# One distance in SBUF between the packed matmul operands and the weights, a shifted last row tile in two of them, and five-bank PSUM for the first three MLP blocks

## The chip, the cores and the metric

The kernel runs on one core of a Trainium2 chip. The metric is the device time of one execution in microseconds (us); ns are nanoseconds. Engines are named as in the profile: PE is TensorE's matmul, PEld its weight load, DVE is VectorE, ACT is ScalarE, POOL is GpSimd, SP is SyncE, whose queue issues the weight DMAs.

## The reference

One decoder layer on 256 tokens and 16 prepended meta tokens, width 2048, in fp32. The parts that matter here:

```python
proj = xn @ w_in                    # xn = rmsnorm(h); 11 pieces: q, k, v of both mixers, gates
o_fox = forgetting_attention(...)   # 8 heads of 128: 1024 channels
o_gla = head_rmsnorm(gated_linear_attention(...)) * silu(gr)        # 2048 channels
y = sigmoid(gate_fox) * (o_fox @ w_o_fox) + sigmoid(gate_gla) * (o_gla @ w_o_gla)
h = h + y @ w_out
h = h + square(relu(rmsnorm(h) @ w_ff1)) @ w_ff2                    # d_ff = 8192
return rmsnorm(h)[:, 16:]
```

## The kernel before, in words

Activations lie transposed: 128 channels on the partitions, tokens along the row. A weight matrix is cut into blocks of 2048 input by 128 output channels (1 MB), and the blocks are streamed from HBM in the order in which they are used, in two halves of 8 row tiles of 128x128. Each half is copied by ACT to `whi` (rounded to TensorE's fp32r) and DVE writes the remainder `wlo` (L120, L121). Five buffers of 4096 bytes each serve `raw`, `whi` and `wlo`.

A product to fp32 accuracy takes three matmuls in fp32r: hi by hi, hi by the operand's remainder, remainder of the weights by hi. `gemm3` does so for one output block: 16 row tiles `k`, for each of them L144 (`whi`, operand half 0), L145 (`whi`, half 1), L146 (`wlo`, half 0). That is 48 matmuls with 256 columns and 48 weight loads, in one PSUM bank. The banks come from pool `pg` (three banks in turn); pool `px` (five banks) serves the small products.

Five operands of `gemm3` are made by `operand`: a row tile takes 512 floats (2048 bytes), the layout is row tile, token half, hi or remainder, 128 tokens. Argument `at` says at which float of the SBUF tile the packed data start. They live in two slots (tags `s1`, `s2`) and, for `of`, in pool `late`:

- `of`, 8 row tiles: attention's output; `og`, 16 row tiles: the linear attention's output. A loop over `j0` makes eight passes; a pass has four gate blocks (`gate`, with `gemm2` and the operand `x`, L136 and L137; for the first pass they come ahead of the loop), two blocks of 24 matmuls with `of`, two blocks of 48 with `og`.
- `y`, 16 blocks with `w_out`; each block's result is added to `h`, and from it row tile `j` of `x2` is made and squared for the second norm.
- MLP: four groups `g`; in each 16 blocks with `x2` (w_ff1), whose squared relu fills `a`, then 16 blocks with `a` (w_ff2). In the last group the last four blocks are done in another way (L917, L933).

`x2` holds h times the norm's gain but not its root: the squared relu `relu2` multiplies by `r2b` (L883), the root that `norm2` makes while the first MLP block runs. Until then the first results wait in their PSUM banks.

A scheduler sets the order of each engine's queue. On PE the `gemm3` blocks follow each other as in the source, but for the first pass, where it interleaves them, since the corners of `of` (the last 16 tokens of each half, `fill_corners`, L805 to L809) come late.

Of the kernel before, what the change touches and what calls it, by code (L numbers as in the profile page):

```python
# [7 lines left out]
F32 = mybir.dt.float32  # L8
F32R = mybir.dt.float32r
# [7 lines left out]
P = 128  # L17
D = 2048
KT = D // P
NM = 16  # L20
NT = 256
NA = NM + NT
EPS = 1e-6
FOX_H, FOX_D = 8, 128
# [10 lines left out]
O_FQ, O_FK, O_FV, O_FF = 0, 1024, 2048, 3072  # L35
O_GQ, O_GK, O_GV, O_GR = 3080, 4104, 5128, 7176
O_GA, O_GF, O_GG = 9224, 9240, 11288


def stream():  # L40
# [25 lines left out]
def trunk(ctx: ExitStack, tc: tile.TileContext, hT, w_small, w_all, consts, w_alpha2, out):  # L66
# [3 lines left out]
    def nm(s):  # L70
        serial[0] += 1
        return f"{s}_{serial[0]}"

    const = ctx.enter_context(tc.tile_pool(name="const", bufs=1))
    keep = ctx.enter_context(tc.tile_pool(name="keep", bufs=1))
# [3 lines left out]
    pg = ctx.enter_context(tc.tile_pool(name="pg", bufs=3, space=PSUM))  # L79
    px = ctx.enter_context(tc.tile_pool(name="px", bufs=5, space=PSUM))  # L80
# [3 lines left out]
    def bank(pool, s):  # L84
        return pool.tile([P, 512], F32, tag="bank", name=nm(s))
# [7 lines left out]
    def issued():  # L93
        for e in list(waiting):
            e[0] -= 1
            if e[0] <= 0:
                waiting.remove(e)
                e[1]()
# [9 lines left out]
    def weight_half(c, i, hi=None):  # L108

        raw = wp.tile([P, HK * P], F32, tag="raw", name=nm("raw"), bufs=RAW)  # L110
        if hi is None:
            hi = wp.tile([P, HK, P], F32R, tag="whi", name=nm("whi"))
        lo = wp.tile([P, HK, P], F32R, tag="wlo", name=nm("wlo"))

        def step(k0, n):
            k = slice(k0, k0 + n)
            cols = slice(k0 * P, (k0 + n) * P)
            nc.sync.dma_start(raw[:, cols], w_all[c][:, i * HK * P + cols.start : i * HK * P + cols.stop])
            r = raw.rearrange("p (k m) -> p k m", m=P)[:, k, :]
            nc.scalar.copy(hi[:, k, :], r)  # L120
            nc.vector.tensor_tensor(lo[:, k, :], r, hi[:, k, :].bitcast(F32), op=ALU.subtract)  # L121

        return hi, lo, step

    def next_weights(keep_hi=None):
        c = chunk[0]
        chunk[0] += 1
        parts = []
        for i in range(2):
            hi, lo, step = weight_half(c, i, None if keep_hi is None else keep_hi[:, HK * i : HK * (i + 1), :])  # L130
            step(0, HK)
            parts.append((hi, lo))
        return lambda k: (parts[k // HK][0][:, k % HK, :], parts[k // HK][1][:, k % HK, :])
# [2 lines left out]
        nc.tensor.matmul(ps, hi, x, start=first, stop=False)  # L136
        nc.tensor.matmul(ps[:, 0:NT], lo, x[:, 0, :], start=False, stop=last)  # L137

    def gemm3(w, x, k0=0, nk=KT):

        ps = bank(pg, "ps")[:, 0:NT]
        for k in range(nk):
            hi, lo = w(k0 + k)
            nc.tensor.matmul(ps, hi, x[:, k, 0], start=(k == 0), stop=False)  # L144
            nc.tensor.matmul(ps, hi, x[:, k, 1], start=False, stop=False)  # L145
            nc.tensor.matmul(ps, lo, x[:, k, 0], start=False, stop=(k == nk - 1))  # L146
        issued()
        return ps

    def gemm2(w, x, k0=0, nk=KT):  # L150

        ps = bank(pg, "ps")
        for k in range(nk):
            hi, lo = w(k0 + k)
            mac2(ps, hi, lo, x[:, k], k == 0, k == nk - 1)
        issued()
        return ps

    def gemm_all(w):

        ps = bank(pg, "psa")
        for k in range(KT):
            hi, lo = w(k)
            nc.tensor.matmul(ps[:, 0:NA], hi, x_hi[:, k], start=(k == 0), stop=False)  # L164
            nc.tensor.matmul(ps[:, 0:NA], lo, x_hi[:, k], start=False, stop=(k == KT - 1))  # L165
            nc.tensor.matmul(ps[:, X_LO], hi, x_lo[:, k], start=False, stop=(k == KT - 1), skip_group_check=True)  # L166
        join(ps)
        issued()
        return ps
# [6 lines left out]
    def total(ps, t=None):  # L176

        b = tmp.tile([P, NT], F32, tag="evb", name=nm("evb"))
        nc.scalar.copy(b, ps[:, NT:512])
        if t is None:  # L180
            t = tmp.tile([P, NT], F32, tag="evt", name=nm("evt"), bufs=4)
        nc.vector.tensor_tensor(t, ps[:, 0:NT], b, op=ALU.add)
        return t

    def split_to(dst_hi, dst_lo, src):
        nc.scalar.copy(dst_hi, src)
        nc.vector.tensor_tensor(dst_lo, src, dst_hi.bitcast(F32), op=ALU.subtract)
# [38 lines left out]
            nc.vector.scalar_tensor_tensor(r, r, -0.5, v, op0=ALU.mult, op1=ALU.mult)  # L226
            nc.vector.scalar_tensor_tensor(y, r, 1.5, y, op0=ALU.add, op1=ALU.mult)

    def operand(pool, name, nk=KT, at=0, **kw):

        t = pool.tile([P, nk * (2 * NT + 32)], F32R, name=nm(name), **kw)
        return t[:, at : at + nk * 2 * NT].rearrange("p (k a o t) -> p k o a t", a=2, o=2, t=P)

    def pair(ap):
        return ap.rearrange("p (a t) -> p a t", t=P)
# [6 lines left out]
    x = x_row[:, :, NM : NM + 2 * NT].rearrange("p k (o t) -> p k o t", t=NT)  # L242
# [3 lines left out]
    ident, scan = cons[:, 0:P], cons[:, P : P + NA]  # L246
    ggn, ba, bf = cons[:, 400:416], cons[:, 416:424], cons[:, 424:425]

    room = keep.tile([P, KT * 2 * NT], F32, tag="s2", name="room")
    at_room = [0]  # L250

    def take(*shape):
# [55 lines left out]
    def load_stage(s, part):  # L308
        c0, n = ((0, 4), (4, 3))[part]
        w = first_weights(c0, n, 2 * s)  # L310
        stages.setdefault(s, []).append(w)
        return w[2](0, n) if s else w[2]
# [14 lines left out]
    for s in range(KT // 2):  # L327
        if s + 3 < KT // 2:
            with tc.issue_after(load_stage(s + 3, 0).ins):
                load_h(nc.sync, 2 * s + 6, 2)  # L330
            last = load_stage(s + 3, 1).ins
        wa, wb = stages[s]
        for kk in range(2):
            k = 2 * s + kk
# [15 lines left out]
        at = [(w[0][:, c], w[1][:, c]) for w, n in ((wa, 4), (wb, 3)) for c in range(n)]  # L350
# [38 lines left out]
    for i in range(2):  # L389
        w = wp.tile([P, HK, P], F32R, tag="whi", name=nm("whi"))  # L390
# [269 lines left out]
    ps = bank(pg, "psa")  # L660
    for k in range(KT):
        if k == HK:
            norm1()
        w = small[k // HK][:, k % HK, :]
# [28 lines left out]
    cum.close()  # L693
    branches = ExitStack()
    late = branches.enter_context(tc.tile_pool(name="late", bufs=1, reuse_waits="tile"))
    of = operand(late, "of", FOX_H, 96)
    negc = late.tile([P, FOX_H, NA], F32, name="negc")
    nc.gpsimd.dma_start(negc.rearrange("p h t -> p (h t)"), fdram.to_broadcast([P, FOX_H * NA]))
    fox = ExitStack()
# [16 lines left out]
    def fox_head(hd):  # L716
        fk = att.tile([P, NA], F32, tag="fk", name=nm("fk"))
        fq = att.tile([P, NT], F32, tag="fq", name=nm("fq"))
        ps = gemm_all(next_weights())
        nc.vector.tensor_tensor(fk, ps[:, 0:NA], rb, op=ALU.mult)  # L720
        t = total(gemm2(next_weights(), x))
# [32 lines left out]
        ps = gemm_all(next_weights())  # L754
# [11 lines left out]
        vg, pgr, og4 = corner["v"], corner["p"], corner["o"]  # L766
# [38 lines left out]
        def fill_corners(pu, vz, pz):  # L805
            nc.tensor.matmul(pu[:, 2 * P : 3 * P], vz, pz, start=True, stop=True)
            nc.vector.tensor_tensor(og4, og4, pu[:, 2 * P : 3 * P].rearrange("p (h c q) -> p h c q", c=2, q=NM),
                                    op=ALU.add)
            split_to(*(of[:, hd - 3 : hd + 1, o, :, P - NM :] for o in range(2)), og4)  # L809

        later(1, turn_v)
        later(2, turn_p)
# [20 lines left out]
    for j0 in range(0, KT, 2):  # L833
        gates = ahead if j0 == 0 else [gate() for _ in range(4)]
        w = next_weights()
        for j in range(2):
            t = gemm3(w, of, k0=8 * j, nk=8)
            nc.vector.tensor_tensor(gates[2 * j], gates[2 * j], t, op=ALU.mult)
        for j in range(2):
            t = tmp.tile([P, NT], F32, tag="evt", name=nm("evt"), bufs=4)  # L840
            nc.vector.tensor_tensor(t, gates[2 * j + 1], gemm3(next_weights(), og), op=ALU.mult)
            nc.vector.tensor_tensor(yf[:, j0 + j, :], gates[2 * j], t, op=ALU.add)
    y = operand(keep, "y", at=96, tag="s1")
    for j in range(KT):
        split_to(y[:, j, 0], y[:, j, 1], pair(yf[:, j, :]))
    mix.close()
# [6 lines left out]
    x2 = operand(keep, "x2", at=64, tag="s2")  # L853

    def square_sum(j, acc):
        if j == 0:
            nc.scalar.activation(acc, ht[:, j, :], AF.Square)
        else:
            sq = gat.tile([P, NT], F32, tag="hsq", name=nm("hsq"))
            nc.scalar.activation(sq, ht[:, j, :], AF.Square)  # L860
            nc.gpsimd.tensor_tensor(acc, acc, sq, op=ALU.add)

    def add_residual(j, ps):
        nc.vector.tensor_tensor(ht[:, j, :], ps, ht[:, j, :], op=ALU.add)
# [16 lines left out]
    def relu2(a, f, ps):  # L881
        t = tmp.tile([P, NT], F32, tag="evt", name=nm("evt"), bufs=4)
        nc.vector.scalar_tensor_tensor(t, ps, 0.0, r2b, op0=ALU.max, op1=ALU.mult)  # L883
        s = gat.tile([P, NT], F32, tag="asq", name=nm("asq"))
        nc.vector.tensor_tensor(s, t, t, op=ALU.mult)
        split_to(a[:, f, 0], a[:, f, 1], pair(s))

    acc = gat.tile([P, NT], F32, tag="acc", name="acc3", bufs=1)
    for g in range(NG):
        a = operand(keep, "a", at=(96, 64, 80, 64)[g], tag="s1")  # L890
        held = []
        for f in range(KT):
            ps = gemm3(next_weights(), x2)
            if g == 0 and f == 0:
                held.append(ps)
                continue
            if g == 0 and f == 1:
                relu2(a, 0, held.pop())
            relu2(a, f, ps)
        last = g == NG - 1  # L900
        for j in range(KT - NL if last else KT):
            add_residual(j, gemm3(next_weights(), a))
            if last:
                square_sum(j, acc)
                nc.scalar.activation(ht[:, j, :], ht[:, j, :], AF.Identity, scale=gain(2, j))
                if j == 0:
                    tc.keep_in_program_order(nc.scalar.preload_act_table_set("natural_log_exp_and_others"))
# [5 lines left out]
    for n in range(NL):  # L913
        j, ps = KT - NL + n, bank(pg if n < 3 else px, "ps")
        w = next_weights(whi[:, n])
# [148 lines left out]
```

## Time and profile before

| | |
|---|---|
| median of 3 runs | 1590.02 us (1589.83, 1590.02, 1592.55) |
| the profiled execution's own time | 1592.38 us |
| its span | 1590.7 us, 30310 instructions |
| PE busy | 1580.0 us (99%), 12436 matmuls |
| PEld busy | 1533.7 us (96%), 12436 weight loads |
| DVE, ACT, POOL busy | 1003.6 us (63%), 747.1 us (47%), 126.9 us (8%) |
| HBM | 289.32 MB read, 183 GB/s over the span |
| granted TensorE clock | 0.998 |

Matmuls overlap in the trace: one of 256 columns is shown with some 280 ns, while the next starts some 115 ns after it. How fast PE goes is therefore read from how many matmuls start in a stretch of time, or from how long a stage with a known number of matmuls lasts, and not from the duration of one. The windows that are cut at the first matmul of a stage give this directly: 16 blocks of `gemm3` are 768 matmuls.

### The profile page before, as it was taken

The page shows a single profiled execution, that of the slowest core. Times are in us where ns is not written, and L with a number is a line of the kernel's source. Part 1 is how long each engine was busy: PE and PEld are TensorE (multiplying, and loading weights), DVE is VectorE, ACT ScalarE, POOL GpSimd, SP SyncE. Part 2 cuts the span into 40 slices and gives each one's busy share as a digit, 9 for nine tenths or more (in the row PEclk, how much of TensorE's full clock was granted, in tenths as well). Part 3 has the DMA queues.
Part 4 walks back from the last instruction along what each step waited for, and adds up shares of the span by engine and source line. Part 5 has one row for each costly group of instructions (what it writes and reads, how often), then busy time and mean ns, then how long its engine had stood idle before and what let it go on. Part 6 is the DMA issues. An engine that isn't in the chain of part 4 may idle for free.

```text
span 1590.7 us, 30310 instructions
## 1 busy us (share of the span) xinstructions
PE 1580.0 (99%) x12436; PEld 1533.7 (96%) x12436; DVE 1003.6 (63%) x1487; ACT 747.1 (47%) x1099; POOL 126.9 (8%) x213
## 2 busy tenths in 40 slices
PE   9999999999999999999999999999999999999997
PEld 8999999999999999999999999999999999999997
DVE  7897757676665555555666765556655665556655
ACT  7665444455544444444544443344433443344553
POOL 6021000011100000000011000000000000000022
PEclk9999999999999999999999999999999999999999
DMA  9454545555545555556555555556656655556652
GB/s 325 153 167 151 182 159 179 167 188 165 164 162 183 188 193 190 189 187 194 188 187 186 186 186 186 186 190 195 195 192 197 192 193 185 184 188 196 192 184 106
DMA packets 86619, 293.41 MB, mean 184 GB/s; under 512 B 9112, under 2 KB 16800, under 8 KB 86352
## 3 DMA queue, kind: packets, MB, share of 16 engines
q1 hardware_dynamic: 85872, 289.62, 56.4%
q8 instruction: 98, 1.61, 0.4%
q0 software_dynamic: 176, 1.12, 0.2%
q10 hardware_dynamic: 432, 0.72, 0.1%
q14 instruction: 41, 0.34, 0.1%
HBM read 289.32 MB, written 2.11 MB: 183 GB/s over the span
## 4 chain that ended last, share of the span: by engine, by line
PE 98%; DMA 0%; DVE 0%; issue 0%; ACT 0%; POOL 0%; SPq 0%; POOLq 0%; ACTq 0%
PE ps L145 19%; PE ps L144 19%; PE ps L146 19%; PE ps L136 13%; PE ps L137 7%; PE psa L166 5%; PE psa L165 5%; PE psa L164 5%; PE ps L356 1%; PE ps L933 1%; PE ps L361 1%; PE pa L559 1%; PE ps L917 0%; DMA raw<-w_all_dram 0%; PE po L622 0%
## 5 line engine op out<-in xcount | busy, mean ns | idle before, releaser
L121 DVE TENSOR_TENSOR wlo<-raw,whi 128x1024 fp32r<-128x1024 f32 x522 | 640.9, 1228 | 420.1 <-ACT whi L120 411.0
L120 ACT CAST whi<-raw 128x1024 fp32r<-128x1024 f32 x522 | 548.5, 1051 | 699.9 <-PE ps L145 484.3
L136 PE MATMUL ps<-x,whi 128*128 128x512 f32 x928 | 326.9, 394 | 0.0
L144 PE MATMUL ps<-x,whi 128*128 128x256 f32 x1024 | 284.0, 277 | 0.5 <-DVE evt L883 0.5
L146 PE MATMUL ps<-x,wlo 128*128 128x256 f32 x1024 | 284.0, 277 | 0.0
L145 PE MATMUL ps<-x,whi 128*128 128x256 f32 x1024 | 284.0, 277 | 0.0
L145 PE MATMUL ps<-a,whi 128*128 128x256 f32 x960 | 268.0, 279 | 0.0
L146 PE MATMUL ps<-a,wlo 128*128 128x256 f32 x960 | 267.8, 279 | 0.0
L144 PE MATMUL ps<-a,whi 128*128 128x256 f32 x960 | 267.8, 279 | 0.0
L137 PE MATMUL ps<-x,wlo 128*128 128x256 f32 x928 | 261.0, 281 | 0.0
L136 PEld LDWEIGHTS ps<-x,whi 128*128 128x128 f32 x928 | 174.1, 188 | 37.0
L144 PEld LDWEIGHTS ps<-x,whi 128*128 128x128 f32 x1024 | 193.2, 189 | 0.6 <-issue 0.6
L145 PEld LDWEIGHTS ps<-x,whi 128*128 128x128 f32 x1024 | 192.3, 188 | 0.0
L146 PEld LDWEIGHTS ps<-x,wlo 128*128 128x128 f32 x1024 | 192.3, 188 | 0.0
L144 PEld LDWEIGHTS ps<-a,whi 128*128 128x128 f32 x960 | 181.5, 189 | 0.0
L164 PE MATMUL psa<-x,whi 128*128 128x272 f32 x624 | 181.4, 291 | 0.0
L145 PEld LDWEIGHTS ps<-a,whi 128*128 128x128 f32 x960 | 181.4, 189 | 0.0
L166 PE MATMUL psa<-x,whi 128*128 128x272 f32 x624 | 181.2, 290 | 0.0
L146 PEld LDWEIGHTS ps<-a,wlo 128*128 128x128 f32 x960 | 181.2, 189 | 0.0
L165 PE MATMUL psa<-x,wlo 128*128 128x272 f32 x624 | 179.5, 288 | 0.0
L137 PEld LDWEIGHTS ps<-x,wlo 128*128 128x128 f32 x928 | 175.3, 189 | 0.1
L164 PEld LDWEIGHTS psa<-x,whi 128*128 128x128 f32 x624 | 118.2, 189 | 0.4
(313 smaller groups left out, 2207.3 us busy)
## 6 DMA issues: line engine op xcount, KB each, us to landing
raw<-w_all_dram SPq DMA_DIRECT2D x537, 512.0 KB, 4.0
raw<-w_all_dram SPq DMA_DIRECT2D x8, 384.0 KB, 6.4
h<-hT_dram SPq DMA_DIRECT2D x8, 275.0 KB, 6.7
negc<-fdram POOLq DMA_DIRECT2D x1, 1088.0 KB, 8.4
out_dram<-o SPq DMA_DIRECT2D x2, 512.0 KB, 2.6
raw<-w_all_dram SPq DMA_DIRECT2D x2, 256.0 KB, 3.7
room<-w_small_dram SPq DMA_DIRECT2D x1, 320.0 KB, 7.7
out_dram<-o ACTq DMA_DIRECT2D x1, 320.0 KB, 3.1
```

What stands on the lines that cost most here:

```text
L120: nc.scalar.copy(hi[:, k, :], r)
L121: nc.vector.tensor_tensor(lo[:, k, :], r, hi[:, k, :].bitcast(F32), op=ALU.subtract)
L136: nc.tensor.matmul(ps, hi, x, start=first, stop=False)
L137: nc.tensor.matmul(ps[:, 0:NT], lo, x[:, 0, :], start=False, stop=last)
L144: nc.tensor.matmul(ps, hi, x[:, k, 0], start=(k == 0), stop=False)
L145: nc.tensor.matmul(ps, hi, x[:, k, 1], start=False, stop=False)
L146: nc.tensor.matmul(ps, lo, x[:, k, 0], start=False, stop=(k == nk - 1))
L164: nc.tensor.matmul(ps[:, 0:NA], hi, x_hi[:, k], start=(k == 0), stop=False)
L165: nc.tensor.matmul(ps[:, 0:NA], lo, x_hi[:, k], start=False, stop=(k == KT - 1))
L166: nc.tensor.matmul(ps[:, X_LO], hi, x_lo[:, k], start=False, stop=(k == KT - 1), skip_group_check=True)
L356: nc.tensor.matmul(ps, hi, x[:, k], start=st, stop=False)
L361: nc.tensor.matmul(ps[:, 0:NT], lo, x[:, k, 0], start=False, stop=sp)
```

## The change

Four edits, all in how tiles lie in memory.

1. `operand` takes as much room as it needs (`at` plus the row tiles, plus `kick`), where it took 32 spare floats for each row tile. With `kick=32` the last row tile starts 32 floats (128 bytes) further than the others. `Rows` hides this from the callers: index `k` picks the one access pattern or the other.
2. `at` and `kick` are set so that all rows stand at one distance from the weights. Here, a distance is the address of a matmul's moving operand less that of its weights, modulo 512 bytes; a weight tile's row is 512 bytes long and an operand's row tile 2048, so it is the same for all row tiles of an operand.

| operand | slot | `at` before, after | distance before, after (bytes) |
|---|---|---|---|
| `of` | `late` | 96, 96 | 192, 192; last row tile 320 |
| `og` | `s2` | 64, 64 | 192, 192 |
| `y` | `s1` | 96, 64 | 320, 192; last row tile 320 |
| `x2` | `s2` | 64, 64 | 192, 192 |
| `a`, group 0 | `s1` | 96, 64 | 320, 192 |
| `a`, group 1 | `s1` | 64, 64 | 192, 192 |
| `a`, group 2 | `s1` | 80, 64 | 256, 192 |
| `a`, group 3 | `s1` | 64, 64 | 192, 192 |

   Slot `s2` becomes 1536 bytes smaller (`og` and `x2` need less, `room` is given 128 floats more), and the weight buffers and all that lies behind them move down by 1536 bytes, three times 512. `x` stays where it is. Modulo 512 no other distance changes.
3. The first three blocks of the MLP take their PSUM bank from `px`; the following ones find the three banks of `pg` free.
4. `fill_corners` splits each of its four heads by itself, since the row tile's index must be one number for `Rows`.

```diff
+class Rows:
+    def __init__(self, most, last):
+        self.most, self.last, self.n = most, last, most.shape[1]
+        self.shape = [most.shape[0], self.n + 1, *most.shape[2:]]
+    def __getitem__(self, at):
+        p, k, *rest = at
+        if k < self.n:
+            return self.most[(p, k, *rest)]
+        return self.last[(p, 0, *rest)]
...
-    def gemm3(w, x, k0=0, nk=KT):
-        ps = bank(pg, "ps")[:, 0:NT]
+    def gemm3(w, x, k0=0, nk=KT, pool=None):
+        ps = bank(pool or pg, "ps")[:, 0:NT]
...
-    def operand(pool, name, nk=KT, at=0, **kw):
-        t = pool.tile([P, nk * (2 * NT + 32)], F32R, name=nm(name), **kw)
-        return t[:, at : at + nk * 2 * NT].rearrange("p (k a o t) -> p k o a t", a=2, o=2, t=P)
+    def operand(pool, name, nk=KT, at=0, kick=0, **kw):
+        t = pool.tile([P, at + nk * 2 * NT + kick], F32R, name=nm(name), **kw)
+        def rows(k, n, at):
+            return t[:, at + k * 2 * NT : at + (k + n) * 2 * NT].rearrange("p (k a o t) -> p k o a t", a=2, o=2, t=P)
+        return Rows(rows(0, nk - 1, at), rows(nk - 1, 1, at + kick)) if kick else rows(0, nk, at)
...
-    room = keep.tile([P, KT * 2 * NT], F32, tag="s2", name="room")
+    room = keep.tile([P, KT * 2 * NT + P], F32, tag="s2", name="room")
...
-    of = operand(late, "of", FOX_H, 96)
+    of = operand(late, "of", FOX_H, at=96, kick=32)
...
-            split_to(*(of[:, hd - 3 : hd + 1, o, :, P - NM :] for o in range(2)), og4)
+            for i in range(4):
+                split_to(*(of[:, hd - 3 + i, o, :, P - NM :] for o in range(2)), og4[:, i])
...
-    y = operand(keep, "y", at=96, tag="s1")
+    y = operand(keep, "y", at=64, kick=32, tag="s1")
...
-        a = operand(keep, "a", at=(96, 64, 80, 64)[g], tag="s1")
+        a = operand(keep, "a", at=64, tag="s1")
...
-            ps = gemm3(next_weights(), x2)
+            ps = gemm3(next_weights(), x2, pool=px if g == 0 and f < 3 else pg)
```

What moves in the engines' queues is the corners alone. ACT's queue at the last corners (`of` is written from the tile `og4`, shown as `og`), before:

```order
L120 COPY whi_6043<-raw_6042 128x1024
L179 COPY evb_5901<-ps_5864 128x256
L186 COPY of_3715<-og_764_4925 128x8x16
L825 ACTIVATE gate_5906<-evt_5903 128x256
L120 COPY whi_6049<-raw_6048 128x1024
```

and ACT's queue at the same place now:

```order
L133 COPY whi_6055<-raw_6054 128x1024
L192 COPY evb_5913<-ps_5870 128x256
L199 COPY of_3715<-og_764_4925 128x2x16 x4
L843 ACTIVATE gate_5918<-evt_5915 128x256
L133 COPY whi_6061<-raw_6060 128x1024
```

One copy has become four smaller ones at the same place of the queue; the remainders on DVE likewise. PE's queue in the first pass, where the second half of the `of` blocks follows a stretch of `og` matmuls (`ps_5990` and `ps_6002` are the same bank of an `og` block), before:

```order
L144 MATMUL ps_5990<-og_1416,whi_5979 128x256
L145 MATMUL ps_5990<-og_1416,whi_5979 128x256
L146 MATMUL ps_5990<-og_1416,wlo_5980 128x256
L145 MATMUL ps_5925<-of_3715,whi_5914 128x256
L146 MATMUL ps_5925<-of_3715,wlo_5915 128x256
```

and PE's queue there now:

```order
L157 MATMUL ps_6002<-og_1416,whi_5991 128x256
L158 MATMUL ps_6002<-og_1416,whi_5991 128x256
L158 MATMUL ps_5937<-of_3715,whi_5926 128x256
L159 MATMUL ps_5937<-of_3715,wlo_5927 128x256
L157 MATMUL ps_5937<-of_3715,whi_5926 128x256
```

One `og` matmul has moved behind the `of` matmuls, so that these stand one place earlier. All other queues have their instructions in the same order.

## The prediction

> **What bounds the kernel now.** I read the page first: busy time, clock, and the chain that ended last.
>
> ```profile
> PE 1580.0 (99%) x12436; PEld 1533.7 (96%) x12436; DVE 1003.6 (63%) x1487; ACT 747.1 (47%) x1099; POOL 126.9 (8%) x213
> PEclk9999999999999999999999999999999999999999
> PE 98%; DMA 0%; DVE 0%; issue 0%; ACT 0%; POOL 0%; SPq 0%; POOLq 0%; ACTq 0%
> ```
>
> PE is the bound from end to end, at the full granted clock, and waits for next to nothing. The change takes no matmul away, so all it can do is alter how fast matmuls follow each other. The busy share doesn't tell that. The stage table does: here are the windows cut at the first matmul of `y`, `x2` and `a` of group 0, `x2` and `a` of group 1, both of group 2, and `x2` of group 3, each 16 blocks of 48, so 768 matmuls of 256 columns (the counts are 2 to 5 higher, since a matmul that began earlier and the norm's two are included). Columns after the window: its length, then busy us and count of PE, PEld, DVE, ACT, POOL, then clock, DMA share, GB/s.
>
> ```profile
> 781.41:871.87 90.46, 90.46 (x771) 90.46 (x770) 59.52 (x65) 44.75 (x63) 14.03 (x14) 1.00 0.59 192
> 871.87:962.65 90.78, 90.32 (x773) 90.15 (x772) 62.70 (x92) 39.85 (x50) 0.99 (x1) 1.00 0.58 186
> 962.65:1053.10 90.45, 90.45 (x770) 90.45 (x769) 46.79 (x50) 33.91 (x33) 0.00 (x0) 1.00 0.58 187
> 1053.10:1140.15 87.05, 87.05 (x771) 87.05 (x769) 57.44 (x78) 38.86 (x47) 0.00 (x0) 1.00 0.61 194
> 1140.15:1227.19 87.04, 87.04 (x771) 87.04 (x769) 46.79 (x50) 34.09 (x33) 0.00 (x0) 1.00 0.60 194
> 1227.19:1314.23 87.04, 87.04 (x771) 87.04 (x769) 57.42 (x78) 38.85 (x47) 0.00 (x0) 1.00 0.61 194
> 1314.23:1406.37 92.14, 92.14 (x771) 92.14 (x770) 46.78 (x50) 33.87 (x33) 0.00 (x0) 1.00 0.58 184
> 1406.37:1493.43 87.06, 87.06 (x771) 87.06 (x770) 57.44 (x78) 38.86 (x47) 0.00 (x0) 1.00 0.61 193
> ```
>
> The same work takes three times: 87.04 us (113.3 ns a matmul) at distance 192, 90.45 us (117.8 ns) at 320 (`y`, `a` of group 0), 92.14 us (120.0 ns) at 256 (`a` of group 2). Clock, count and the DVE and ACT work don't explain it: `a` of groups 0, 1 and 2 has the same 46.8 us of DVE and comes out at all three. DVE's 57 and ACT's 45 us leave room under 87, so no other engine binds at the faster rate.
>
> The exception is the second row: `x2` of group 0 stands at 192 and is slow. Its inside, cut at its one wait:
>
> ```profile
> 871.87:888.34 16.47, 16.47 (x147) 1.00 0.59 190
> 889.08:962.65 73.57, 73.57 (x625) 1.00 0.58 186
> ...
> 888.34 0.28 PE L146 MATMUL ps<-x,wlo 128*128 128x256 f32 x1
> 889.08 0.35 PE L144 MATMUL ps<-x,whi 128*128 128x256 f32 x1 [0.46 <-DVE evt L883]
> 889.27 0.28 PE L145 MATMUL ps<-x,whi 128*128 128x256 f32 x1
> ```
>
> Ahead of the wait some 144 matmuls took 16.47 us (114.4 ns, with the norm's matmuls and the entry). Behind it some 624 took 73.57 us, 117.9 ns, until the stage's end. So 192 has a fast and a slow course, and a course once taken lasts. The passes over `of` and `og`, all at 192, show it again; windows of passes 2 to 8 without their gate blocks, 144 matmuls each:
>
> ```profile
> 530.85:547.81 16.96, 16.96 (x146) 1.00 0.59 189
> 570.11:586.43 16.32, 16.32 (x147) 1.00 0.60 195
> 608.72:625.68 16.96, 16.96 (x147) 1.00 0.58 186
> 647.98:664.30 16.32, 16.32 (x147) 1.00 0.61 192
> 686.58:703.55 16.97, 16.97 (x147) 1.00 0.59 185
> 725.84:742.16 16.32, 16.32 (x146) 1.00 0.60 194
> 764.45:781.41 16.96, 16.96 (x146) 1.00 0.49 160
> ```
>
> They alternate: after a fast pass and its gates comes a slow one, and the reverse. The gate blocks between them cost the same either way:
>
> ```profile
> 508.56:530.85 22.29, 22.29 (x131) 1.00 0.60 202
> 547.81:570.11 22.30, 22.30 (x131) 1.00 0.58 191
> ```
>
> What resets a course is leaving a worse distance: `x2` starts fast behind `y` at 320 although the pass before `y` was slow, it is fast at once behind `a` of group 0 (320) although `x2` had been slow before that, and fast behind `a` of group 2 (256). The rows at the first of these places:
>
> ```profile
> 871.63 0.28 PE L145 MATMUL ps<-y,whi 128*128 128x256 f32 x1
> 871.75 0.28 PE L146 MATMUL ps<-y,wlo 128*128 128x256 f32 x1
> 871.87 0.28 PE L144 MATMUL ps<-x,whi 128*128 128x256 f32 x1
> 871.98 0.28 PE L145 MATMUL ps<-x,whi 128*128 128x256 f32 x1
> 872.10 0.28 PE L146 MATMUL ps<-x,wlo 128*128 128x256 f32 x1
> 872.21 0.28 PE L144 MATMUL ps<-x,whi 128*128 128x256 f32 x1
> ```
>
> Starts go from 0.12 us apart to 0.11 within three matmuls. The shifted last row tile, three matmuls at 320, is such an exit in small.
>
> **The change part by part**, against the profiled execution's own 1592.38 us.
>
> *Stages that come to 192.* `y` goes from 90.46 to 87.04, -3.42 us; `a` of group 0 from 90.45 to 87.04, -3.41; `a` of group 2 from 92.14 to 87.04, -5.10. This needs the fast course at entry. A fast course passes a stage border: `x2` to `a` to `x2` from 1053 to 1314 us without one slow stage.
>
> *The wait in the MLP.* The fourth block starts at 888.34 in the bank that holds block 1, and block 1 waits for `r2b`. With blocks 1 to 3 in `px`, block 4 finds a `pg` bank that `y` left over 10 us before. The next bank to be used twice is that of block 4, by block 7, three blocks (16 us) later, when DVE has long had `r2b`. So the wait goes and nothing is late next. `x2` of group 0 comes to the 87.06 us of group 3: -3.72, of which 0.74-0.11 is the wait itself and the rest the slow course behind it. What lies between blocks 1 and 2, the norm's two matmuls, didn't lose the fast course before.
>
> *Passes.* The four of 16.96 us come to 16.32: 4 x (16.96 - 16.32) = -2.56. But the gates lead from a fast pass to a slow start, and now each of passes 2 to 8 follows a fast one. So its first `of` block, 24 matmuls up to the shifted row, is slow: 7 x 24 x 4.5 ns = +0.75 (bounds 0 and, if the shifted rows don't help, all seven passes at 16.96, 7 x 0.64 = +4.5 against 16.32).
>
> *The shifted rows* cost 3 matmuls at 117.8 and up to 3 more on the way back, 14 to 27 ns, in 16 blocks of `of` and 16 of `y`: 0.45 to 0.86, taken as +0.70.
>
> *The corners.* Four small copies for one. The nearest rows:
>
> ```profile
> L186 ACT CAST of<-og x2: 301/306/312, 417.4 to 493.3; 128x128 fp32r<-128x128 f32 x2
> L187 DVE TENSOR_TENSOR of<-og,of x2: 284/284/284, 418.7 to 494.7; 128x128 fp32r<-128x128 f32 x2
> L793 ACT COPY og<-pof 128x32 f32<-128x32 f32 x8 | 1.5, 186 | 7.7 <-DVE of L187 7.7
> L625 DVE TENSOR_TENSOR po<-po,so 128x32 f32<-128x32 f32 x8 | 1.4, 192 | 0.0
> 497.23 0.28 PE L145 MATMUL ps<-of,whi 128*128 128x256 f32 x1
> ```
>
> 4 x 186 - 306 = 0.44 us more on ACT, 4 x 192 - 284 = 0.48 on DVE, twice. At the last corners DVE's remainder was done at 494.7 + 0.28 = 495.0, and the first matmul that reads it starts at 497.23. It stands one place (0.11 us) earlier now. The 0.9 us fit into the 2.1 that are left: 0. Without that cover the whole would cost 0.9 us once.
>
> *The smaller slot.* The weights move by 1536 bytes against `x`, three times 512. Within one stage the distance modulo 1024 already takes both values in turn, since weights step by 512 and operands by 2048 from one row tile to the next, and the stage is even. So 0, with 1.5 us to either side for what I can't see in the 490 us with `x`.
>
> Sum: 3.42 + 3.41 + 5.10 + 3.72 + 2.56 - 0.75 - 0.70 = 16.76 us, and 1592.38 - 16.76 = 1575.6. The median shown is 1590.02, and the other runs are 1589.83 and 1592.55: two levels 2.6 us apart, about 13 blocks by (90.45 - 87.04) / 16 = 0.21 us, which is what the slow course behind the MLP's wait costs. If the lower level is a run that kept the fast course, the time after is the same 1575.6; if the difference is elsewhere, some 1573.
>
> **Rivals.** *The slow course sticks.* Before, the worse distances of `y` and of `a` in groups 0 and 2 put the matmuls back on the fast course three times. Now nothing between the end of `y` and the end of the kernel does. If PE enters `x2` on the slow course, because three matmuls at 320 are too few for a reset or the last shifted row itself knocks a fast course over, all eight MLP stages take 90.45: 8 x 3.41 = 27.3, so 1602.9 us, slower by 0.8%. It decides at the fourth stage: the gain against the median, 14.4 us, is used up if 14.4 / 3.41 = 4.2 stages are slow. For it: the course behind the wait lasted 70 us; every reset seen came after hundreds of matmuls at the worse distance. Against it: every exit from 320 or 256 that the trace shows ends fast, and the stages from 1053 to 1314 and from 1406 on have no wait that could start it.
>
> *The shifted row toggles.* It resets a slow course and upsets a fast one, so every second block of `y` is slow (8 x 0.21 = 1.7 us) and half of `og` (16 blocks, so 8 x 0.21 = 1.7): 1579.0 us. For it: gates do toggle the passes.
>
> *Distance does nothing*, and what the table shows comes from something that the change leaves alone. Then the wait alone goes: 1592.38 - 0.63 = 1591.7. The Trainium skill says so in "TensorE: Matmul & The Clock Gate", section "Step-by-step: what each phase is for": PE reads the moving operand and the weights through two independent ports, and loading the next weights doesn't steal bandwidth from the running matmul. By that rule the three rates wouldn't exist; this trace disagrees, with 113.3, 117.8 and 120.0 ns at three distances.
>
> **How the numbers follow.** Forecast 0.66: all stages from `y` on fast. Toggling 0.14. Sticking 0.14, anywhere from 1580 (late) to 1602.9. No effect 0.03. The other 0.03 are the unseen effects of the moved buffers. A measurement of this kernel can tell about 0.2% (3.2 us) from no change. Faster by more: 0.66 + 0.14 + half of the last 0.03, and a late sticking, 0.82; within: 0.04; slower: 0.14. The range goes from the forecast with the lower level and the buffers' 1.5 us in its favour, 1572.5, over toggling to 1585, where the sticking would begin to bite: about 8 in 10.
>
> **What would show it.** Stage windows: `y` near 87.4, all eight of the MLP at 87.0 to 87.1; no wait of L144 for `evt`; passes 2 to 8 at some 16.4 with a slow first `of` block (2.83 instead of 2.72 us). A stage of the MLP at 90.4 with nothing that it waited for is the sticking; blocks of `y` that alternate between 5.44 and 5.65 are the toggling. The forecast is wrong if `y` or `a` of group 2 keep their time at 192, or if a new wait appears behind block 4.

## The result, and the profile after

| | before | after |
|---|---|---|
| median | 1591.28 us (4 runs; 1590.02 when the forecast was made) | 1575.48 us (1575.06 to 1576.51, 4 runs) |
| profiled execution, span | 1592.38, 1590.7 us | 1575.57, 1573.9 us |
| ratio of the mean times | | 0.9886, 95% interval 0.9839 to 0.9933 |

1575.6 us was forecast. "Course" is the prediction's word for one of the two rates that matmuls at distance 192 keep, 113.3 ns from start to start (fast) or 117.8 (slow). The runs of the kernel before are spread wider than those of the kernel after, over three levels, which the section on why comes back to.

The stage windows of the kernel after, cut as those of before (`y`, `x2` and `a` of group 0, then `a` of group 2; window, length, busy us and count of PE, PEld, DVE, ACT, POOL, clock, DMA share, GB/s):

```profile
779.74:867.09 87.35, 87.35 (x771) 87.35 (x770) 59.50 (x66) 44.83 (x63) 14.02 (x14) 1.00 0.61 200
867.09:954.39 87.30, 87.30 (x772) 87.30 (x771) 62.65 (x92) 39.93 (x50) 1.00 (x1) 1.00 0.58 192
954.39:1041.43 87.04, 87.04 (x770) 87.04 (x769) 46.80 (x50) 34.09 (x33) 0.00 (x0) 1.00 0.60 195
...
1302.55:1389.59 87.04, 87.04 (x770) 87.04 (x769) 46.81 (x50) 34.09 (x33) 0.00 (x0) 1.00 0.59 196
```

The stages of the MLP behind `x2` of group 0 all run at 113.3 ns a matmul (87.04 / 768), the four that are left out here as well. `x2` of group 0 takes 0.26 us more, and the norm's two matmuls lie in it. `y` pays 0.31 us for its 16 shifted rows, 19 ns each. PE is busy through all of `x2` of group 0: the wait is gone. The list of what PE waited for, whole:

```profile
PE warm L339 <- DVE ones L219: 1.3, 1, 1.3
PE pn L975 <- ACT sq L956: 0.7, 1, 0.7
```

Passes 2 and 8 over `of` and `og`, and pass 2 cut into its first `of` block and its second one:

```profile
530.80:547.25 16.45, 16.45 (x146) 1.00 0.58 190
763.28:779.74 16.46, 16.46 (x147) 1.00 0.49 157
...
530.80:533.62 2.82, 2.82 (x26) 1.00 0.57 192
533.62:536.37 2.75, 2.75 (x27) 1.00 0.60 186
```

No pass is at 16.96 us any more. The first block of a pass is still slow, 2.82 us. The shifted row at its end is the reset: the second block takes 2.75, of which 0.03 is the price of its own shifted row, and `og` behind it is fast. The slow block shows in its weight loads too, where the first of each row tile has a mean of 192 ns and the other two 188 (window 530.90 to 533.50 us; busy us, mean ns); a later experiment comes back to this:

```profile
L157 PEld LDWEIGHTS ps<-of,whi 128*128 128x128 f32 x7 | 1.3, 192 | 0.0
```

The last corners, the four copies and four remainders as one row each, and the first matmul that reads them:

```profile
493.25 0.57 ACT L199 CAST of<-og 128x32 fp32r<-128x32 f32 x4
494.59 1.05 DVE L200 TENSOR_TENSOR of<-og,of 128x32 fp32r<-128x32 f32 x4
497.02 0.28 PE L158 MATMUL ps<-of,whi 128*128 128x256 f32 x1
```

They end at 495.64, 1.4 us ahead of PE.

### The profile page after: what moved, and what is told of

It reads as the page before. It is cut to its first block, busy times and chain, and to the rows that moved or that the text cites. A ratio compares the mean times of both kernels' runs of the same rounds, so it can differ in the third digit from the quotient of the medians.

```text
span 1573.9 us, 30316 instructions
## 1 busy us (share of the span) xinstructions
PE 1564.2 (99%) x12436; PEld 1518.3 (96%) x12436; DVE 1004.3 (64%) x1493; ACT 747.9 (48%) x1105; POOL 126.8 (8%) x213
## 4 chain that ended last, share of the span: by engine, by line
PE 99%; POOL 0%; issue 0%; DVE 0%; POOLq 0%; ACT 0%; ACTq 0%
PE ps L157 19%; PE ps L158 19%; PE ps L159 19%; PE ps L149 13%; PE ps L150 7%; PE psa L179 5%; PE psa L178 5%; PE psa L177 5%; PE ps L373 1%; PE ps L378 1%; PE ps L951 1%; PE pa L576 1%; PE ps L935 0%; PE po L639 0%; PE warm L339 0%
## 5 line engine op out<-in xcount | busy, mean ns | idle before, releaser
L157 PE MATMUL ps<-x,whi 128*128 128x256 f32 x1024 | 282.6, 276 | 0.0
L157 PE MATMUL ps<-a,whi 128*128 128x256 f32 x960 | 265.0, 276 | 0.0
L158 PE MATMUL ps<-a,whi 128*128 128x256 f32 x960 | 265.0, 276 | 0.0
L157 PEld LDWEIGHTS ps<-x,whi 128*128 128x128 f32 x1024 | 192.2, 188 | 0.0
L177 PE MATMUL psa<-x,whi 128*128 128x272 f32 x624 | 181.2, 290 | 0.0
L157 PEld LDWEIGHTS ps<-a,whi 128*128 128x128 f32 x960 | 180.2, 188 | 0.0
L177 PEld LDWEIGHTS psa<-x,whi 128*128 128x128 f32 x624 | 118.1, 189 | 0.4
```

## The experiments

Each kernel is the one after with one edit, unless it says otherwise.

### No shifted row

```diff
-    of = operand(late, "of", FOX_H, at=96, kick=32)
+    of = operand(late, "of", FOX_H, at=96)
-    y = operand(keep, "y", at=64, kick=32, tag="s1")
+    y = operand(keep, "y", at=64, tag="s1")
```

> The changed kernel with no shifted row tile in of and y; all else as changed. Theory (a course at 192 lasts until a worse distance resets it): the passes alternate again, 16.32 and 16.96 us (+1.6 against the changed kernel in sum), the last pass is slow, so y (90.45 us, +3.1) and all eight MLP stages (90.45 each, +27) are slow: some 1607 us. Rival 1, the norm's two matmuls at 320 inside x2 of group 0 are reset enough: only y and the first MLP block are slow, some 1580 us. Rival 2, the shifted rows do nothing: 1575 us.

1608.1 us (1607.69 to 1608.52, 8 runs), ratio to before 1.009 (1.0061 to 1.0118): slower than the kernel before. The passes alternate again, 16.97 us (pass 2) and 16.32 (pass 3). Stage windows (`y`, `x2` of groups 0 and 3):

```profile
782.18:872.64 90.46, 90.46 (x771) 1.00 0.57 191
872.64:963.33 90.69, 90.69 (x772) 1.00 0.56 187
...
1415.60:1506.05 90.45, 90.45 (x771) 1.00 0.55 186
```

From `y` to the end, all at distance 192 and all slow. So the distance alone isn't enough: 192 allows the fast course and doesn't bring it. The rival of the forecast that ended slower, 1602.9 us, is real in a kernel one edit away, and the 96 matmuls at 320 in `of` and `y` are what keeps it out of the kernel after. The norm's two matmuls are no reset here.

### The old banks

```diff
-            ps = gemm3(next_weights(), x2, pool=px if g == 0 and f < 3 else pg)
+            ps = gemm3(next_weights(), x2, pool=pg)
```

> The changed kernel with every MLP block in the three banks of pg again. Theory: the wait of 0.63 us at the fourth block returns and knocks the matmuls onto the slow course, which nothing ends: 13 blocks of x2 of group 0 (+2.7) and seven stages of 90.45 instead of 87.04 us (+24): some 1602.7 us. Rival 1, the course ends by itself at a stage border: +3.4, some 1579 us. Rival 2, the wait alone returns: 1576.1 us.

Two executions: 1602.79 us, the profiled one (granted clock 0.998, as elsewhere), and 1576.57. The line of the MLP in the profiled one's list of what PE waited for:

```profile
PE ps L157 <- DVE evt L901: 0.5, 1, 0.5
```

and its windows of `x2` and `a` of group 0 and of `x2` of group 3:

```profile
867.11:957.89 90.78, 90.32 (x773) 1.00 0.56 186
957.89:1048.34 90.45, 90.45 (x770) 1.00 0.55 187
...
1410.16:1500.61 90.45, 90.45 (x771) 1.00 0.56 186
```

The theory's number (1602.7) and the number of the rival in which the wait alone returns (1576.1) were both met, once each. In the profiled execution the course changed at the wait, and then stayed for over 600 us; that it did not change in the other is read from its time alone, since that one was not profiled. So, by these two executions, the edit to the banks is worth about 1 us or 27, by chance, in a kernel that has no reset behind that place.

### The banks alone, in the kernel before

```diff
...
-            ps = gemm3(next_weights(), x2)
+            ps = gemm3(next_weights(), x2, pool=px if g == 0 and f < 3 else pg)
```

> The kernel before with the first three MLP blocks in px, nothing else. Theory: x2 of group 0 comes from 90.78 to about 87.06 us since the wait and the slow course behind it are gone; y, a of groups 0 and 2 keep 90.45, 90.45 and 92.14: about 3.7 us under a profiled kernel before, some 1588.7. Rival, only the wait itself goes: 0.6 us less, 1591.7, and x2 of group 0 stays at 90.2.

1588.87 us (1588.57 to 1589.06, 8 runs), ratio 0.9966 (0.9939 to 0.9993). Windows of `y`, `x2` and `a` of group 0, `a` of group 2:

```profile
781.48:871.94 90.46, 90.46 (x771) 1.00 0.57 190
871.94:959.25 87.31, 87.31 (x773) 1.00 0.57 193
959.25:1049.70 90.45, 90.45 (x771) 1.00 0.56 187
...
1310.82:1402.97 92.15, 92.15 (x771) 1.00 0.54 183
```

As the theory had it: the second stage gives back 3.5 us, the others keep their time. Eight runs lie within 0.5 us, where the kernel before, run beside it, fell at 1589.4 to 1590.2 (5 of 15), 1592.0 to 1593.2 (7) and 1602.4 to 1602.5 (3). All of that spread goes with the banks, and so with the wait that they cause.

### Other distances, a map

```diff
-    y = operand(keep, "y", at=64, kick=32, tag="s1")
+    y = operand(keep, "y", at=16, tag="s1")
-        a = operand(keep, "a", at=64, tag="s1")
+        a = operand(keep, "a", at=(32, 48, 112, 128)[g], tag="s1")
```

> The changed kernel with y at distance 0 (no shift), a of groups 0 to 3 at 64, 128, 384 and 448; x2 stays at 192. Theory (the two reads of PE disturb each other by their distance, worst near 256): each of these stages has a rate of its own, not above the 120.0 ns a matmul of 256 (92.14 us a stage), 128 and 384 nearer to it than 0 and 448; one or more may lie under 113.3 ns (87.04 us). x2 behind a worse stage starts fast. Rival (distance does nothing by itself, only the course does): every stage is 87.04 or 90.45 us.

One execution, 1592.09 us. Windows of `y` at 0, then `a` at 64, 128 and 384, and the first twelve blocks (576 matmuls) of `a` at 448:

```profile
779.68:871.82 92.14, 92.14 (x770) 1.00 0.55 187
959.14:1049.60 90.46, 90.46 (x771) 1.00 0.56 187
1136.64:1227.78 91.14, 91.14 (x770) 1.00 0.55 185
1314.85:1405.99 91.14, 91.14 (x770) 1.00 0.55 186
1493.07:1558.35 65.28, 65.28 (x579) 1.00 0.58 193
```

That is 120.0, 117.8, 118.7, 118.7 and 113.3 ns a matmul. With the stages of before (256: 120.0; 320: 117.8), distances 256 bytes apart have one rate. The rival, that only the course counts, falls: 91.14 and 92.14 are neither of its two times. The theory holds in that the distances have rates of their own, none above that of 256. Its order (128 and 384 nearer to 256 than 0 and 448) does not: 0 is as bad as 256. No distance beats 192.

A finer map, between 128 and 256:

```diff
-    y = operand(keep, "y", at=64, kick=32, tag="s1")
+    y = operand(keep, "y", at=68, tag="s1")
-        a = operand(keep, "a", at=64, tag="s1")
+        a = operand(keep, "a", at=(72, 76, 60, 56)[g], tag="s1")
```

> The changed kernel with y at distance 208 (no shift) and a of groups 0 to 3 at 224, 240, 176 and 160; x2 stays at 192. Read with the map before it, in which distances 256 apart gave the same rate (0 and 256: 120.0 ns; 64 and 320: 117.8; 128 and 384: 118.7; 192 and 448: 113.3). Theory (a smooth window around 192 in which the reads miss each other): 176 and 208 stay at 113.3 ns (87.0 us a stage), 160, 224 and 240 rise toward 118 to 120. Rival (192 is a single lucky line of the memory): 176 and 208 are already at 117 or more, 90 us.

One execution, 1597.62 us. Windows of `y` at 208, `a` at 224, `a` at 240, the `x2` stage (192) behind that, `a` at 176, and twelve blocks of `a` at 160:

```profile
779.80:871.32 91.52, 91.52 (x771) 1.00 0.56 189
958.62:1049.50 90.88, 90.88 (x771) 1.00 0.55 186
1136.57:1226.54 89.97, 89.97 (x771) 1.00 0.56 188
1226.54:1316.99 90.45, 90.45 (x771) 1.00 0.55 187
1316.99:1408.58 91.59, 91.59 (x771) 1.00 0.55 185
1495.64:1563.22 67.58, 67.58 (x578) 1.00 0.55 188
```

119.2, 118.3, 117.1, then 119.3 and 117.3 ns. The smooth window falls; the rival was right: 16 bytes to either side of 192 cost 5%. And the fourth row is the first exit from a worse distance that did not end fast: behind 240, a whole `x2` stage took 90.45 us. The prediction's "every exit ends fast" was a statement on 320 and 256 alone. In the weight loads of this stage the second of each row tile is the long one (40 us from 1250 us; the other two have 188 ns):

```profile
L158 PEld LDWEIGHTS ps<-x,whi 128*128 128x128 f32 x114 | 21.9, 192 | 0.0
```

The same distances entered from the slow course, with no shifted rows and `a` at 448, 208, 176 and 192:

```diff
-    of = operand(late, "of", FOX_H, at=96, kick=32)
+    of = operand(late, "of", FOX_H, at=96)
-    y = operand(keep, "y", at=64, kick=32, tag="s1")
+    y = operand(keep, "y", at=64, tag="s1")
-        a = operand(keep, "a", at=64, tag="s1")
+        a = operand(keep, "a", at=(128, 68, 60, 64)[g], tag="s1")
```

> The changed kernel without shifted rows, so that y and x2 of group 0 run the slow course (90.45 us each), with a of groups 0 to 3 at 448, 208, 176 and 192. Theory (448 is the same place as 192, half a weight row further): a of group 0 keeps the slow course, 90.45 us, x2 of group 1 too; at 208 or 176 it is seen whether the slow course exists there: if it does, all of the MLP stays near 90.45 a stage and the time is some 1607 us. Rival (only 192 has a slow course, or 208 or 176 are reset by themselves): the stage at that distance and all behind it come to 87.04 us: 3.4 us less for each stage behind the first reset, so between 1584 and 1604 us.

One execution, 1600.81 us, within the rival's range. Windows of `a` at 448, `a` at 208, and the `x2` behind that:

```profile
963.73:1054.18 90.45, 90.45 (x770) 1.00 0.56 186
...
1144.64:1236.16 91.52, 91.52 (x771) 1.00 0.55 185
1236.16:1323.22 87.06, 87.06 (x771) 1.00 0.58 194
```

448 keeps the slow course as 192 does. 208 has its one rate, 91.52, from either side, and leaving it is a reset. 176 has 91.59 in this kernel, entered from the fast course, and in the finer map, entered from a slow one. So of the distances tried, 192 and 448 alone have the fast course. Of those entered from both a fast and a slow stage (128, 176, 192 with 448, 208 and 320), 192 alone has two; 0 and 256, 160, 224 and 240 were entered from a fast stage only, so a second rate there isn't ruled out.

### The distance, or the operand's own address?

So far the weights had stood at one address modulo 256, so the maps couldn't tell.

```diff
-    room = keep.tile([P, KT * 2 * NT + P], F32, tag="s2", name="room")
+    room = keep.tile([P, KT * 2 * NT + P + 16], F32, tag="s2", name="room")
-    y = operand(keep, "y", at=64, kick=32, tag="s1")
+    y = operand(keep, "y", at=80, tag="s1")
-        a = operand(keep, "a", at=64, tag="s1")
+        a = operand(keep, "a", at=80, tag="s1")
```

> The changed kernel with all weight buffers 64 bytes further (16 floats more in the slot before them), y (no shift) and a moved by 64 bytes as well, x2 and og left where they were. So y and a have their distance of 192 kept and their address moved, x2 and og have their address kept and stand at 128. Theory (the distance between the two counts): y and a of all groups at 87.04 us a stage, the x2 stages at 91.14, as 128 was in the map. Rival (the operand's own address counts, whatever the weights' is): x2 stays at 87.04 or 90.45 us, y and a go to the rate that 256 had, 92.14.

One execution, 1600.66 us. Windows of `y`, `a` of group 0, `x2` of group 1:

```profile
784.39:874.84 90.45, 90.45 (x771) 1.00 0.58 190
...
966.20:1053.28 87.08, 87.08 (x771) 1.00 0.59 193
1053.28:1144.42 91.14, 91.14 (x771) 1.00 0.57 186
```

`x2` was not moved and its time changed to that of 128; `a` was moved with the weights and kept its own. The distance counts. (`y`, which came behind `og` at 128, took the slow course of 192; that was not foreseen. It is the second exit that did not end fast. `a` of group 0, which came behind `x2` at the same 128, was fast, so the distance that is left doesn't decide alone.) This bears on a page of the Trainium skill once more: "SBUF — State Buffer", section "Who interferes with whom", has it that PE never waits on anyone at SBUF. The trace of before agrees in that another engine's work does not explain the rates (`a` of groups 0, 1 and 2 had 46.8 us of DVE and 33.9 to 34.1 of ACT at three rates). But the distance between PE's own two operands does matter: moving it by 64 bytes, from 192 to 128, cost 4.10 us, 4.7% of a stage.

### Rows of `x` at one distance

`x` has rows of 2176 bytes, so that its distance changes by 128 from row tile to row tile. Rows of 2304 bytes, nine times 256, hold it still:

```diff
-    x_row = keep.tile([P, KT, 2 * NA], F32R, tag="s1", name="x")
+    x_row = keep.tile([P, KT * 576], F32R, tag="s1", name="x").rearrange("p (k c) -> p k c", c=576)
...
```

> The changed kernel with rows of x of 2304 bytes instead of 2176, so that all row tiles of x stand at one distance modulo 256: the 272-column operand at 192, the operand of the gate and query blocks (512 and 256 columns) and the 272 columns of remainders at 0. Before they alternate from row tile to row tile by 128. Theory: the 272-column matmuls at 192 come down by about 5 ns (two of three, 1248 of them: -6 us), those at 0 stay within 2 ns; some 1570 us. Rival (the distance matters only for 256 columns, or changes of distance cost nothing): 1575.5 us.

1574.04 us (1573.77 and 1574.32), ratio to before 0.987 (0.9768 to 0.9972): 1.4 us under the median of the kernel after, a quarter of what the theory had; the two were not timed side by side. Pass 2, which takes 16.45 us in the kernel after, here:

```profile
530.66:547.03 16.37, 16.37 (x147) 1.00 0.57 193
```

The gain is not where the theory had it. The stretch with the 272-column matmuls is 1.1 us shorter (415.7 us from the first start of L177 to the last, 416.8 in the kernel after), where 6 were forecast, and this execution had lost most of that ahead of it and behind: the gates of pass 2 begin at 508.47 against 508.51 us. The gates take 0.1 us less and the pass behind them 0.08, since its first `of` block is fast now (2.74 us); seven times both is the 1.3 us that part the profiled executions (1574.32 and 1575.57 us).

And 192 bytes further, so that the gates' operand is at 192:

```diff
-    x_row = keep.tile([P, KT, 2 * NA], F32R, tag="s1", name="x")
+    x_row = keep.tile([P, KT * 576 + 64], F32R, tag="s1", name="x")[:, 48 : 48 + KT * 576].rearrange(
+        "p (k c) -> p k c", c=576)
...
```

> As the run with rows of x of 2304 bytes, with x started 192 bytes further: the 512- and 256-column operand and the 272 columns of remainders at 192, the 272-column operand at 128. Theory: a 512-column matmul comes from 232.8 to about 220 ns (twice 106.7 and the 6.6 that 113.3 has over 106.7), its 256-column one from 117.6 to 113.3, 928 of each: up to -15.8 us; the 272-column remainders -2.5, the other 272-column ones 0 to +5: some 1560 to 1565 us, less of a gain where pauses put the matmuls on the slow course. Rival (a 512-column matmul isn't disturbed since it is twice as long as the weight load): -4 to -6 us, some 1570.

1580.66 us (1580.26 to 1581.25, 8 runs): 5 us slower than the kernel after, where theory and rival both had a gain. In the profiled execution 2.9 us of it lie ahead of the gates of pass 2 (they begin at 511.45 instead of 508.51 us; the stretch with the 272-column matmuls is 2.4 us longer), and the gates take 0.31 us more in each of seven passes. Four gate blocks of pass 2 in the kernel after, with distances 0 and 128 in turn, then with 0, then with 192:

```profile
508.51:530.80 22.29, 22.29 (x131) 1.00 0.60 198
```

```profile
508.47:530.66 22.19, 22.19 (x130) 1.00 0.61 208
```

```profile
511.45:534.05 22.60, 22.60 (x131) 1.00 0.60 203
```

A pair of 512 and 256 columns has the opposite order: 0 is better than 192 (22.19 / 64 = 346.7 ns a pair against 353.1). A distance found for one sequence of matmuls does not hold for another.

### The shifted row first

```diff
-    of = operand(late, "of", FOX_H, at=96, kick=32)
+    of = operand(late, "of", FOX_H, at=96, first=32)
...
+        if first:
+            return FirstRow(rows(0, 1, at - first), rows(1, nk - 1, at))
```

> The changed kernel with the first row tile of each of-block at 320 instead of the last. Theory: the reset comes at the start of a pass's first of-block, which falls from 2.83 to about 2.74 us in seven passes: -0.6 us, some 1574.9. Rival (a shifted first row is entered from the gates' course and doesn't reset): passes 2 to 8 start slow and stay so, +0.5 us a pass, and the last one hands its slow course on to y, whose own shift ends it: some 1580 us.

1583.08 us (1582.58 to 1583.93, 10 runs), ratio to before 0.9924 (0.9895 to 0.9953): the rival's direction, and worse than it. The row stood at 64, which is 320 less 256. A later kernel put it at 320 itself, as a ninth row tile:

```diff
-            return FirstRow(rows(0, 1, at - first), rows(1, nk - 1, at))
+            return FirstRow(rows(nk, 1, at + first), rows(1, nk - 1, at))
...
```

> As the run with the first row tile of each of-block shifted, where the shifted row stood at 64 (320 less 256); now it stands at 320 itself, behind the other rows. Theory (the same as 64, and the place in the block decides: entered straight from the gates' course, three matmuls leave a slow course whose long weight load is the third of a row tile, which a shifted last row doesn't end): all passes slow, y at 90.45 us, some 1583 us. Rival (64 was the fault, 320 resets): the first of-blocks at 2.74 us, y at 87.35, some 1574.9.

1583.15 us, `y` and the passes as in the run before it, so 64 was not the fault. Windows of pass 2, `y` and `x2` of group 0 with the row at 64:

```profile
531.42:548.38 16.96, 16.96 (x147) 1.00 0.56 188
783.86:874.31 90.45, 90.45 (x771) 1.00 0.58 189
874.31:961.84 87.53, 87.53 (x773) 1.00 0.59 193
```

All of `y` is slow, although each of its 16 blocks still ends with a row at 320. And here `x2` comes to the fast course by itself, in the blocks around the norm's matmuls. In the kernel after, such a row ended a slow course, and in the kernel with no shifted row the norm's matmuls ended none. The weight loads tell the two apart; PEld's groups over 40 us of `y` (from 800 us; busy us, mean ns), here:

```profile
L172 PEld LDWEIGHTS ps<-y,wlo 128*128 128x128 f32 x114 | 21.8, 192 | 0.0
L170 PEld LDWEIGHTS ps<-y,whi 128*128 128x128 f32 x114 | 21.4, 188 | 0.0
L171 PEld LDWEIGHTS ps<-y,whi 128*128 128x128 f32 x113 | 21.2, 188 | 0.0
```

and in the kernel with no shifted row:

```profile
L157 PEld LDWEIGHTS ps<-y,whi 128*128 128x128 f32 x113 | 21.7, 192 | 0.0
L158 PEld LDWEIGHTS ps<-y,whi 128*128 128x128 f32 x114 | 21.4, 188 | 0.0
L159 PEld LDWEIGHTS ps<-y,wlo 128*128 128x128 f32 x114 | 21.4, 188 | 0.0
```

On the slow course one weight load in three takes 192 ns instead of 188, and which of the three it is stays as it is: the first of a row tile (L157) in the one kernel, the third (L172) in the other. They are slow courses of the same rate. Three matmuls at 320 ended the kind with the first load long (the first `of` blocks of the kernel after) and not the kind with the third (`y` here). The kind with the second load long is the `x2` stage behind 240 above, at the same 90.45 us; the `x2` stage after that, behind `a` at 176, is fast again (87.06 us from 1408.58).

### Together

Rows of `x` of 2304 bytes, the first row of `of` shifted (at 64), no shift in `y`:

> Together: rows of x of 2304 bytes, the shifted row first in the of-blocks, no shift in y. Theory: the 1574.0 us of the run with those rows, less 0.6 for the of-blocks and 0.3 for y's 16 shifts: some 1573.1, y at 87.05 us. Rival (y and the MLP need the reset at y's end, since og hands over a slow course or the norm's matmuls make one): y or the MLP's stages at 90.45, some 1577 to 1604 us.

1573.22 us (1572.84 to 1573.87, 4 runs), ratio to before 0.9855 (0.9806 to 0.9905). Windows of the gates and the rest of pass 2, of `y`, of `x2` of group 0:

```profile
507.45:529.64 22.19, 22.19 (x131) 1.00 0.61 200
529.64:546.00 16.36, 16.36 (x147) 1.00 0.60 195
777.32:864.36 87.04, 87.04 (x771) 1.00 0.61 201
864.36:951.66 87.30, 87.30 (x773) 1.00 0.58 192
```

Its median is 2.3 us under that of the kernel after; the two were not timed side by side. The profiled executions are 2.7 us apart, and the stages account for it: gates 0.1 us in each of seven sets, passes 0.1 in seven, `y` 0.3, and 1.1 ahead of the gates of pass 2, where the stretch with the 272-column matmuls is 1.2 us shorter. The same shifted first row that left the passes slow above leaves them fast here: with `x` at one distance the gates hand over the fast course, as the first `of` block of the run with those rows showed (2.74 us). Whether any shifted row is still needed with them was not tried.

## Why the prediction was right

Point by point, in the order of its sum, from the profiled executions:

| term | forecast | measured |
|---|---|---|
| `y`, with its shifts (-3.42, +0.35) | -3.07 | 90.46 to 87.35: -3.11 |
| `a` of group 0 | -3.41 | 90.45 to 87.04: -3.41 |
| `a` of group 2 | -5.10 | 92.14 to 87.04: -5.10 |
| `x2` of group 0 | -3.72 | 90.78 to 87.30: -3.48 |
| passes 2 to 8 (-2.56, +0.75, +0.35) | -1.46 | 116.81 to about 7 x 16.46: -1.6 |
| corners, moved buffers | 0 | what is left of the sum: -0.1 |
| sum | -16.76 | 1592.38 to 1575.57: -16.81 |

`x2` of group 0 was mis-sized by 0.24: I took the time of group 3's, which has no norm matmuls in it. The shifted rows cost 19 ns each in `y`, between the bounds of 14 and 27. The corners took 0.57 us on ACT and 1.05 on DVE, where four copies of 186 ns and four remainders of 192 ns, 0.74 and 0.77, were taken from the nearest rows; 1.4 us of cover were left.

The mechanism, two courses at one distance and a reset by matmuls at 320, is shown by four kernels: no shifted row (slow to the end), old banks (the wait can start the slow course), banks alone, and the entry at 448. It is not a rule for every worse distance: behind 240, and once behind 128, matmuls at 192 were slow. Two steps of the reasoning were weaker than they read. "Every exit from 320 or 256 ends fast" came from stages that were wholly at the worse distance, and the three matmuls of a shifted row are not the same: there is a kind of slow course that they do not end, and the kernel after works since its passes begin with the kind that they do. That was luck; nothing in the prediction told the kinds apart. And the rival that the slow course sticks, at 0.14, was worked out right (1602.9 us; 1608.1 with the passes and `y`, and 1602.79, were measured in kernels one edit away); the gain of this kernel hangs on 96 matmuls at a worse distance and on the absence of a wait.

The three levels of the kernel before: 1589 is the time of the banks-alone kernel (1588.9) plus the 0.6 us wait, and 1592 the profiled course with its 13 slow blocks (+2.7). That agrees with the numbers; only the second was profiled. The third, 1602.4, is 10.2 us above the second, which is three stages of 3.41: those between `a` of group 0 and `a` of group 2. A slow course that outlasts `a` of group 0 would explain it. No execution at that level was profiled, so this stays open. So does why one distance in 256 bytes has two courses: the traces show starts and weight loads and nothing of the reads themselves.

The rival that distance does nothing had 0.03, and it fell: by the rule of the Trainium skill that stood beside it ("TensorE: Matmul & The Clock Gate", section "Step-by-step: what each phase is for", on the two independent read ports) equal matmuls would have one rate, and at nine distances modulo 256 the runs show rates from 113.3 to 120.0 ns.

## What to carry to other kernels

Where PE is busy all the time, read the time from start to start of equal matmuls, stage by stage: here the few per cent between stages of equal work came from how the operands lay and from how the stage was entered, and from no other engine. Try the moving operand's distance from the weights over 256 bytes, in steps of 16 bytes (here the good place was gone 16 bytes to either side), in the very sequence of matmuls that is to run, since another width can want another place; and look at every rate twice, once entered from a fast stage and once from a slow one. If a rate has two courses, plan the entry: no wait in the long stretch, and something in front that is known to lead into the good one.

## What the hardware showed that was not expected

- Nine distances of 256-column matmuls, modulo 256 bytes: 0: 120.0 ns, 64: 117.8, 128: 118.7, 160: 117.3, 176: 119.3, 192: 113.3 or 117.8, 208: 119.2, 224: 118.3, 240: 117.1. The good one is gone 16 bytes to either side.
- The rate at 192 has memory: one execution kept 117.8 ns for over 600 us after a wait of some 0.6 us, and by its time (1576.57 us against 1602.79) another execution of the same kernel did not.
- The slow course shows in the weight loads (one in three 192 instead of 188 ns), and which one it is goes with what ends it: three matmuls at 320 ended the kind with the first load long, not the kind with the third.
- Pairs of 512 and 256 columns: 346.7 ns at distance 0, 353.1 at 192, the reverse of the 256-column case.
